# Windowed and neighbourhood attention in one layer: two heads split as one tile, attention output stored in parts and added by transfers, small operations on GpSimd

## The chip, the cores and the metric

The kernel runs on one core of a Trainium2 chip. The metric is device time in microseconds, measured over the whole program; the kernel before was run three times. Beside it stands one profiled execution, whose span is the time from its first to its last instruction. The engines are TensorE (PE in the profile, its weight loads PEld), VectorE (DVE), ScalarE (ACT), GpSimd (POOL) and SyncE (SP), which here only issues transfers.

## The reference

One layer of an encoder on 1024 tokens of 1024 channels, float32. What the change touches is the attention in its middle:

```python
h = x + 0.5 * swiglu(rms_norm(x), ...)
u = rms_norm(h)
qa, ka, va, qb, kb, vb, ga, gb = split(u @ w_in)
ya = neighbourhood_attention_2d(qa, ka, va, rpb)         # branch A: 8 heads of 64, window 8 x 16 on a 64-wide grid, learned bias
yb = windowed_gqa_sink(rope(qb), rope(kb), vb, sink)     # branch B: 8 heads, 2 key heads, |i - j| <= 128, sink logit in the denominator
merged = sigmoid(ga) * (ya @ w_branch_a) + sigmoid(gb) * (yb @ w_branch_b)
h = h + merged @ w_out
h = h + 0.5 * swiglu(rms_norm(h), ...)
y = rms_norm(h, final_norm)
```

Both attentions are a softmax over the window; in branch B `exp(sink)` is added to the sum of the exponentials, with no value behind it.

## The kernel before, in words

**Numbers in two parts.** Matmuls take float32r operands. A float32 operand is split into a high part (a ScalarE cast, L95) and the rest (a VectorE subtraction, L98), and a product is three matmuls: high x high, high x low, low x high (`mm3`, L149, L151, L153). The large products of the two feed-forward halves and of the input projection use one Strassen step each (`products`, `Down`).

**Stages.** First feed-forward half, input projection, attention, merge and output projection, second feed-forward half, final norm. Tokens are reordered on the host so that a block of 128 tokens is a compact piece of the grid; then each query block j needs the key blocks j-1, j and j+1 in both branches.

**A unit of attention.** A unit is one query block (128 tokens) for two heads. Branch B has 8 blocks x 4 pairs = 32 units, branch A 4 pairs x 8 blocks = 32 units, in this order. For a unit:

- `scores` (L1403): for each of the two heads two matmuls (L1417, L1418: queries times the high and low parts of the keys) into one PSUM bank of 384 columns (256 at the edge blocks). VectorE adds the bias or mask, negates and takes the running minimum (L1422), ScalarE takes the exponential and its sum (L1425). In branch B the negated sink logit is copied in as one column ahead of the scores (L1414 for both heads at once, or L1421 one by one in every third unit, whose buffers lie apart). Then VectorE takes the reciprocal of both sums (L1428) and scales one head (L1429), while ScalarE scales the other (L1430).
- `turn` (L1432): six transposes (L1438), three for each head's bank, then `split` of each bank (L95 on ScalarE, L98 on VectorE) into high and low probabilities.
- `values` (L1445): value matmuls into one bank `g` (L1457 for B, L1452 for A) and `write`. The values tile holds the high part in columns 0 to 63 and the low part in 64 to 127, so the upper 64 output partitions are a second addend: ScalarE copies it down (L1361, L1381) and VectorE adds (L1362; in A, where two probability parts give two results, L1382 and L1386 or L1392).

**Where y goes.** For branch B and for the first three head pairs of branch A the sum is stored to a DRAM buffer `y_d` (L1364 from GpSimd's queue, one transfer for a block; L1388 from SP's queue, one for four blocks) and fetched again as rows (`fetch_y`, L1253), then split into operands of the branch projections (`split_y`, L1255). The last head pair of A stays in the chip's memory.

**The order of the work.** A loop over n (L1476) interleaves the units as a pipeline: scores of unit n, some filler, transposes of unit n-2, some filler, values of unit n-3. The filler is a generator of other matmuls (remaining gate columns, then branch B's projection, then the first two tiles of branch A's); `filling` (L1463) takes a number of steps fixed by constants, a step being six 128x512 matmuls. `prep_a` loads the keys, queries and values of branch A's next head pair from GpSimd's queue (L1211, L1214) and SP's (L1221). From this program order a planner makes each engine's own order: it places an instruction by its estimate of when the operands will be there, so that loads go far ahead of their place in the text. Each engine and each queue then runs its list strictly in that order and waits on semaphores. Instructions marked with `pin` (in `split_y` the high cast, `late=True`) keep their program order on their engine. The first stage is ordered by hand and not touched.

**PSUM.** One pool of eight banks: four for tag `g`, four for tag `d`. `bank(tag)` hands out one bank of 512 columns in rotation. Scores take two `d` banks one after the other, transposes the next two.

Of the kernel before, what the change touches and what calls it, by code (L numbers as in the profile page):

```python
# [15 lines left out]
P = 128  # L16
# [6 lines left out]
HD = 64  # L23
# [13 lines left out]
def trunk_kernel(ctx, tc, x, xt, n1, wg1, wu1, wd1, nm, win, rpb, sink, wa, wb, wo,  # L37
# [11 lines left out]
    ps = ctx.enter_context(tc.tile_pool(name="ps", bufs=4, space=bass.MemoryType.PSUM))  # L49
    dram = ctx.enter_context(tc.tile_pool(name="dram", bufs=1, space=bass.MemoryType.DRAM))  # L50

    uid = [0]

    def nm_(s):
        uid[0] += 1
        return f"{s}_{uid[0]}"
# [3 lines left out]
    nhalf4 = const.tile([P, 4], F32, name="nhalf")  # L60
    nc.gpsimd.memset(nhalf4, -0.5)
    nhalf = nhalf4[:, 0:1]

# [16 lines left out]
    def bank(tag):  # L80
        return ps.tile([P, 512], F32, tag=tag, name=nm_(tag))

    def raw4():
        return main.tile([P, 1024], F32, tag="raw", bufs=4, name=nm_("raw"))
# [883 lines left out]
    u_d = dram.tile([4, P, 512], F32, name="u_d")  # L968
    y_d = dram.tile([D, T], F32, name="y_d")
    kept.append(u_d)  # L970
# [209 lines left out]

    drain(pg[2])
    mix["lo"] = main.tile([P, 512], F32, tag="s1", bufs=1, name=nm_("s1")).rearrange("p (k s t) -> p k s t", k=2, s=2)

# [67 lines left out]
    def fetch_y(r0):  # L1251
        mix["y", r0] = raw4()
        nc.sync.dma_start(mix["y", r0], y_d[r0:r0 + P, :])  # L1253

# [11 lines left out]
    def branch_a(i):  # L1266

        bs = [bank("dg"[i % 2]) for _ in range(2)]
        a_mm.append((bs, branch_mm(bs, mix.pop(("w", NC8 + i)), Y_A)))
# [83 lines left out]
    def units_b():  # L1353
        for j in range(NTT):
            for c in range(4):
                def write(o, j=j, c=c):

                    if c == 0:
                        ybox["b"] = xs4()[:HD].rearrange("p (c s t) -> p c s t", c=4, s=2)
                    lo = mix["lo"][:HD, c % 2]  # L1360
                    nc.scalar.copy(lo, o[HD:])  # L1361
                    nc.vector.tensor_tensor(ybox["b"][:, c], o[:HD], lo, op=ALU.add)  # L1362
                    if c == 3:
                        nc.gpsimd.dma_start(y_d[:512, j * P:(j + 1) * P].rearrange("(c s p) t -> p c s t", s=2, p=HD), ybox["b"])  # L1364

                g = c // 2
                yield dict(j=j, q=[qs_b(j)[:, 4 * s + c, :] for s in range(2)],
                           kd=[kd_b()[g]] * 2, kl=[kl_b()[g]] * 2, v=[mix["vb"][g]], bias=[mask_b] * 2,
                           sink=nsk[:, 2 * c:2 * c + 2], write=write)

    def units_a():
        for hp in range(4):
            qs, kd, kl, va = heads_a[hp]
            for j in range(NTT):
                def write(o, j=j, hp=hp):

                    if hp == 3 and j == 0:
                        ybox["a"] = new_fx(2)
                    y = fa[:, 3072:4096] if hp < 3 else ybox["a"]
# [4 lines left out]
                    if hp < 3:  # L1384
                        both = y[j // 4 * HD:j // 4 * HD + HD].rearrange("p (s t) -> p s t", s=2)
                        nc.vector.tensor_tensor(both[:, :, j % 4 * P:(j % 4 + 1) * P], o[:HD, :, 0, :], lo, op=ALU.add)  # L1386
                        if j in (3, 7):
                            nc.sync.dma_start(y_d[512 + hp * P:512 + (hp + 1) * P, cols].rearrange("(s p) t -> p s t", s=2), both)  # L1388
                        return
                    for s in range(2):  # L1390
# [12 lines left out]
    def scores(un):  # L1403
# [9 lines left out]
        if ext and not third:  # L1413
            nc.vector.tensor_copy(both[:, :, 0], un["sink"])  # L1414
        for s in range(2):
            b = bank("d")
            nc.tensor.matmul(b[:, :nw], un["q"][s], un["kd"][s][:, k0 * P:k1 * P], start=True, stop=False)  # L1417
            nc.tensor.matmul(b[:, :nw], un["q"][s], un["kl"][s][:, k0 * P:k1 * P], start=False, stop=True)  # L1418
            pr = held[4 + s][:, :ext + nw] if third else both[:, s, :ext + nw]
            if ext and third:  # L1420
                nc.vector.tensor_copy(pr[:, 0:1], un["sink"][:, s:s + 1])  # L1421
            nc.vector.tensor_tensor_reduce(out=pr[:, ext:], in0=b[:, :nw], in1=un["bias"][s][:, moff:moff + nw], scale=-1.0,  # L1422
# [4 lines left out]
        npair[0] += 1  # L1427
        nc.vector.reciprocal(rc, ssum)  # L1428
        nc.vector.tensor_scalar_mul(un["pr"][0], un["pr"][0], rc[:, 0:1])  # L1429
        nc.scalar.activation(un["pr"][1], un["pr"][1], AF.Copy, scale=rc[:, 1:2])  # L1430

    def turn(un):  # L1432
        nk = un["nk"]
        un["p"] = [ws4()[:, :768].rearrange("p (k s t) -> p k s t", k=3, s=2) for _ in range(2)]
        for s in range(2):
            pt = bank("d")
            for i in range(nk):
                nc.tensor.transpose(pt[:, i * P:(i + 1) * P], un["pr"][s][:, i * P:(i + 1) * P], ident)  # L1438
# [122 lines left out]


    gain = load_gain(n2[0])
    merge = down
# [65 lines left out]
    scale(NTT - 1)  # L1630


# [67 lines left out]
```

## Time and profile before

| | |
|---|---|
| time, median of 3 runs | 1917.81 us (1917.64 to 1918.79) |
| span of the profiled execution | 1915.6 us |
| TensorE, VectorE, ScalarE, GpSimd busy over the span | 99%, 76%, 49%, 16% |
| attention stage (first score to last value matmul) | 917 to 1161 us |
| bytes moved, whole span | 338.57 MB |

In the profile a row of a group names the line, engine and operation, what is written `<-` what is read, the shapes and the count; then the busy time of the group in us and the mean duration of one in ns; then the idle time of the engine just before such instructions and who ended it. Durations of consecutive instructions of one engine can overlap by some tens of ns. Matmul ends are modelled.

### The profile page before, as it was taken

Reading aid. Unit: us, or ns where it says so; the run is one execution under the profiler, and the core shown is the slowest. Engines: PE = TensorE matmul, PEld = TensorE weight load, DVE = VectorE, ACT = ScalarE, POOL = GpSimd, SP = SyncE. Lnnn points to the kernel's source line nnn. Section 1 sums busy time; section 2 is a strip of 40 time slices with the busy share of each in tenths; the row PEclk is TensorE's granted clock in tenths of the full one; section 3 lists DMA queues with packets and bytes.
Section 4 is the critical chain, followed back from the end, with each engine's and each line's share of the span. In section 5 each row is a group of like instructions: output and inputs, shape, how many; then the busy total and the mean of one; then the engine's idle time right before and its main releaser. Section 6 shows DMA issues by size and latency. Waiting matters only on the chain.

```text
span 1915.6 us, 25959 instructions
## 1 busy us (share of the span) xinstructions
PE 1905.7 (99%) x9044; PEld 1597.7 (83%) x9044; DVE 1451.9 (76%) x2545; ACT 947.5 (49%) x1847; POOL 306.5 (16%) x477
## 2 busy tenths in 40 slices
PE   9999999999999999999999999999999999999998
PEld 7888888888888888898898888888888888888886
DVE  8988766668967778755887997999675566569864
ACT  7533444444446543444888983475333333344453
POOL 0012222214400112211112201010110001005111
PEclk9999999999999999999999999999999999999999
DMA  7256656677354277753648978444432323492341
GB/s 269 95 175 217 231 200 219 205 277 284 115 180 141 105 213 236 226 176 127 176 117 228 283 225 309 171 154 133 142 110 97 118 88 110 157 357 86 119 140 61
DMA packets 174211, 338.57 MB, mean 177 GB/s; under 512 B 17280, under 2 KB 79616, under 8 KB 174080
## 3 DMA queue, kind: packets, MB, share of 16 engines
q1 hardware_dynamic: 140752, 235.18, 37.5%
q0 software_dynamic: 32464, 100.69, 15.6%
q8 instruction: 71, 1.16, 0.3%
q10 hardware_dynamic: 864, 1.05, 0.2%
q14 instruction: 60, 0.49, 0.1%
HBM read 230.43 MB, written 108.19 MB: 177 GB/s over the span
## 4 chain that ended last, share of the span: by engine, by line
PE 97%; DVE 1%; DMA 1%; ACT 0%; issue 0%; POOL 0%; SPq 0%; POOLq 0%; DVEq 0%; ACTq 0%
PE g L149 18%; PE g L153 17%; PE g L151 17%; PE d L153 12%; PE d L151 12%; PE d L149 12%; PE d L1438 2%; PE g L1457 1%; PE d L1417 1%; PE g L1452 1%; PE d L1418 1%; PE d L142 1%; DVE ar L98 0%; DMA fx<-in_xt_dram 0%; DMA fx<-v_d 0%
## 5 line engine op out<-in xcount | busy, mean ns | idle before, releaser
L149 PE MATMUL g<-ar,ws 128*128 128x512 f32 x1064 | 404.6, 393 | 0.0
L151 PE MATMUL g<-ar,ws 128*128 128x512 f32 x1064 | 401.8, 390 | 0.0
L153 PE MATMUL g<-ar,ws 128*128 128x512 f32 x1064 | 400.4, 390 | 0.0
L149 PE MATMUL d<-ar,ws 128*128 128x512 f32 x728 | 281.6, 390 | 0.4 <-ACT ar L908 0.4
L151 PE MATMUL d<-ar,ws 128*128 128x512 f32 x728 | 281.1, 389 | 0.6 <-DVE ar L910 0.6
L153 PE MATMUL d<-ar,ws 128*128 128x512 f32 x728 | 281.2, 389 | 0.0
L153 PEld LDWEIGHTS g<-ar,ws 128*128 128x128 f32 x1064 | 199.6, 188 | 41.6
L151 PEld LDWEIGHTS g<-ar,ws 128*128 128x128 f32 x1064 | 199.6, 188 | 41.0
L149 PEld LDWEIGHTS g<-ar,ws 128*128 128x128 f32 x1064 | 196.6, 188 | 35.9 <-DVE fa L1030 0.3
L332 DVE TENSOR_TENSOR ws<-raw,ws 128x512 fp32r<-128x512 f32 x216 | 147.6, 688 | 92.9 <-ACT ws L325 92.0
L325 ACT CAST ws<-raw 128x512 fp32r<-128x512 f32 x216 | 132.6, 620 | 149.6 <-PE g L153 67.0
L151 PEld LDWEIGHTS d<-ar,ws 128*128 128x128 f32 x728 | 136.7, 188 | 29.8 <-DVE ar L910 1.2
L149 PEld LDWEIGHTS d<-ar,ws 128*128 128x128 f32 x728 | 136.5, 188 | 28.9 <-ACT ar L908 0.9
L153 PEld LDWEIGHTS d<-ar,ws 128*128 128x128 f32 x728 | 136.6, 188 | 28.7 <-DVE ws L332 0.5
L95 ACT CAST ws<-raw 128x512 fp32r<-128x512 f32 x98 | 61.0, 623 | 119.2 <-PE d L153 59.9
L98 DVE TENSOR_TENSOR ws<-raw,ws 128x512 fp32r<-128x512 f32 x98 | 73.2, 747 | 44.3 <-ACT ws L95 44.2
L444 POOL DMA_DIRECT2D hid<-fx x91 | 49.2, 540 | 349.6 <-DVE fx L504 221.6
L98 DVE TENSOR_TENSOR ws<-ar,ws 128x512 fp32r<-128x512 f32 x114 | 93.5, 828 | 14.6 <-ACT ws L95 14.6
L95 ACT CAST ar<-raw 128x512 fp32r<-128x512 f32 (+1 forms) x81 | 54.0, 670 | 83.5 <-PE g L151 51.5
L149 PE MATMUL g<-ws,ws 128*128 128x512 f32 x232 | 90.9, 392 | 0.0
L153 PE MATMUL g<-ws,ws 128*128 128x512 f32 x232 | 90.4, 390 | 0.0
L151 PE MATMUL g<-ws,ws 128*128 128x512 f32 x232 | 90.3, 389 | 0.0
(344 smaller groups left out, 3830.9 us busy)
## 6 DMA issues: line engine op xcount, KB each, us to landing
raw<-hid SPq DMA_DIRECT2D x70, 512.0 KB
hid<-fx POOLq DMA_DIRECT2D x91, 256.0 KB, 2.7
ar<-in_ffn_w_down_dram SPq DMA_DIRECT2D x32, 512.0 KB
raw<-in_ffn_w_up_dram SPq DMA_DIRECT2D x31, 512.0 KB
raw<-in_ffn_w_gate_dram SPq DMA_DIRECT2D x27, 512.0 KB
hid<-fa POOLq DMA_DIRECT2D x51, 256.0 KB, 2.7
ar<-zs_d POOLq DMA_DIRECT2D x48, 256.0 KB, 7.5
raw<-in_w_in_dram SPq DMA_DIRECT2D x20, 512.0 KB
```

Of the source, the lines that this page charges most:

```text
L95: hi = nc.scalar.copy(dst_hi, src)
L98: (eng or nc.vector).tensor_tensor(dst_lo, src, f32v(dst_hi), op=ALU.subtract)
L142: nc.tensor.transpose(pt[:, c * P:(c + 1) * P], xs[:, (half * 4 + c) * P:(half * 4 + c + 1) * P], ident)
L149: nc.tensor.matmul(b, lhs[0], r[0], start=first, stop=False, **kw)
L151: nc.tensor.matmul(b, lhs[0], r[1], start=False, stop=False, **kw)
L153: nc.tensor.matmul(b, lhs[1], r[0], start=False, stop=last, **kw)
L325: nc.scalar.copy(w[0][:, :512], a)
L332: nc.vector.tensor_tensor(w[0][:, 512:], a, f32v(w[0][:, :512]), op=ALU.subtract)
L444: nc.gpsimd.dma_start(hid[PRODUCTS.index(p), i], src)
L1417: nc.tensor.matmul(b[:, :nw], un["q"][s], un["kd"][s][:, k0 * P:k1 * P], start=True, stop=False)
L1418: nc.tensor.matmul(b[:, :nw], un["q"][s], un["kl"][s][:, k0 * P:k1 * P], start=False, stop=True)
L1438: nc.tensor.transpose(pt[:, i * P:(i + 1) * P], un["pr"][s][:, i * P:(i + 1) * P], ident)
```

## The change

- The `d` banks move into a second PSUM pool, which is closed and opened again: as four single banks before and after attention, and as two tiles of two banks during attention. The two heads of a unit take the two halves of one tile, in `scores` and in `turn`.
- In branch B the probabilities of both heads are split by one ScalarE copy and one VectorE subtraction over both banks (768 columns) instead of one pair for each head.
- `y_d` gets three layers. Branch B's `write` is now a single ScalarE copy of all 128 partitions; every fourth one issues two transfers, of the upper and the lower 64 partitions, into layers 0 and 1. For the first three head pairs of branch A `write` is one ScalarE copy and one VectorE copy into one of two small boxes, and three transfers from SP's queue into layers 0, 1 and 2, for each block. `fetch_y` loads layer 0 from SP's queue and adds the other layers (one for B, two for A) by accumulating transfers on GpSimd's queue.
- The reciprocal is now a power of -1 on GpSimd; the copies of the sink column are on GpSimd.

```diff
+    second = {}
+    def open_second(pairs):
+        if second:
+            second["guard"].__exit__(None, None, None)
+        second["guard"] = tc.tile_pool(name=f"pd{len(second)}{int(pairs)}", bufs=2 if pairs else 4,
+                                       space=bass.MemoryType.PSUM, reuse_waits="tile")
+        second["pool"] = second["guard"].__enter__()
...
+    none2 = const.tile([P, 2], F32, name="none")
+    nc.gpsimd.memset(none2, -1.0)
+    open_second(False)
...
+    def two_banks():
+        t = second["pool"].tile([P, 1024], F32, tag="d", name=nm_("d"))
+        return t.rearrange("p (s k) -> p s k", s=2)
...
-    y_d = dram.tile([D, T], F32, name="y_d")
+    y_d = dram.tile([3, D, T], F32, name="y_d")
...
     drain(pg[2])
+    open_second(True)
...
     def fetch_y(r0):
-        mix["y", r0] = raw4()
-        nc.sync.dma_start(mix["y", r0], y_d[r0:r0 + P, :])
+        r = mix["y", r0] = raw4()
+        nc.sync.dma_start(r, y_d[0, r0:r0 + P, :])
+        for k in range(1, 2 if r0 < 512 else 3):
+            nc.gpsimd.dma_start(r, y_d[k, r0:r0 + P, :], accum_op=ALU.add)
...
-        bs = [bank("dg"[i % 2]) for _ in range(2)]
+        bs = [bank("g") for _ in range(2)] if i % 2 else [b for b in two_banks().rearrange("p s k -> s p k")]
...
-                        ybox["b"] = xs4()[:HD].rearrange("p (c s t) -> p c s t", c=4, s=2)
-                    lo = mix["lo"][:HD, c % 2]
-                    nc.scalar.copy(lo, o[HD:])
-                    nc.vector.tensor_tensor(ybox["b"][:, c], o[:HD], lo, op=ALU.add)
+                        ybox["b"] = xs4().rearrange("p (c s t) -> p c s t", c=4, s=2)
+                    nc.scalar.copy(ybox["b"][:, c], o)
                     if c == 3:
-                        nc.gpsimd.dma_start(y_d[:512, j * P:(j + 1) * P].rearrange("(c s p) t -> p c s t", s=2, p=HD), ybox["b"])
+                        for k in range(2):
+                            nc.gpsimd.dma_start(y_d[k, :512, j * P:(j + 1) * P].rearrange("(c s p) t -> p c s t", s=2, p=HD),
+                                                halves(ybox["b"])[k])
...
+                    if hp < 3:
+                        box = fa[:, 3072 + j % 2 * 512:][:, :512].rearrange("p (k s t) -> p k s t", k=2, s=2)
+                        nc.scalar.copy(box[:, 0], o[:, :, 0, :])
+                        nc.vector.tensor_copy(box[:HD, 1], o[:HD, :, 1, :])
+                        for k, part in enumerate((box[:HD, 0], box[HD:, 0], box[:HD, 1])):
+                            nc.sync.dma_start(y_d[k, 512 + hp * P:512 + (hp + 1) * P, j * P:(j + 1) * P]
+                                              .rearrange("(s p) t -> p s t", s=2), part)
+                        return
...
-            nc.vector.tensor_copy(both[:, :, 0], un["sink"])
+            nc.gpsimd.tensor_copy(both[:, :, 0], un["sink"])
+        banks = two_banks()
         for s in range(2):
-            b = bank("d")
+            b = banks[:, s]
...
-                nc.vector.tensor_copy(pr[:, 0:1], un["sink"][:, s:s + 1])
+                nc.gpsimd.tensor_copy(pr[:, 0:1], un["sink"][:, s:s + 1])
...
-        nc.vector.reciprocal(rc, ssum)
+        nc.gpsimd.tensor_tensor(rc, ssum, none2, op=ALU.pow)
...
+        banks = two_banks()
         for s in range(2):
-            pt = bank("d")
+            pt = banks[:, s]
...
-            else:
-                dst = [un["p"][k][:, :nk, s, :] for k in range(2)]
-            split(dst[0], dst[1], pt[:, :nk * P].rearrange("p (k t) -> p k t", k=nk))
+                split(dst[0], dst[1], pt[:, :nk * P].rearrange("p (k t) -> p k t", k=nk))
+        if len(un["v"]) == 1:
+            hi, lo = [p[:, :nk].rearrange("p k s t -> p s k t") for p in un["p"]]
+            split(hi, lo, banks[:, :, :nk * P].rearrange("p s (k t) -> p s k t", k=nk))
...
+    open_second(False)
     gain = load_gain(n2[0])
```

The matmuls, their count, and the numbers of filler steps are the same in both kernels.

More of the change, by code (lines that the diff above doesn't have):

```diff
@@ L80, in bank @@
     def bank(tag):
-        return ps.tile([P, 512], F32, tag=tag, name=nm_(tag))
+        return (ps if tag == "g" else second["pool"]).tile([P, 512], F32, tag=tag, name=nm_(tag))
+    def two_banks():
+        t = second["pool"].tile([P, 1024], F32, tag="d", name=nm_("d"))
+        return t.rearrange("p (s k) -> p s k", s=2)
     def raw4():
@@ L1375, in write @@
                 def write(o, j=j, hp=hp):
-                    if hp == 3 and j == 0:
+                    if hp < 3:
[6 more added lines that the diff above has]
+                        return
+                    if j == 0:
                         ybox["a"] = new_fx(2)
-                    y = fa[:, 3072:4096] if hp < 3 else ybox["a"]
+                    y = ybox["a"]
                     lo = mix["lo"][:HD, j % 2]
@@ L1383, in write @@
                     cols = slice((j - 3) * P, (j + 1) * P)
[L1384 to L1389, printed above, removed]
                     for s in range(2):
@@ L1630, in trunk_kernel @@
     scale(NTT - 1)
+    second["guard"].__exit__(None, None, None)
 def _consts():
```

## The prediction

> **What bounds the kernel now.** I read the page first, then the chain of waits, then the stretch in which the changed lines run.
>
> ```profile
> span 1915.6 us, 25959 instructions
> PE 1905.7 (99%) x9044; PEld 1597.7 (83%) x9044; DVE 1451.9 (76%) x2545; ACT 947.5 (49%) x1847; POOL 306.5 (16%) x477
> PE 97%; DVE 1%; DMA 1%; ACT 0%; issue 0%; POOL 0%; SPq 0%; POOLq 0%; DVEq 0%; ACTq 0%
> ```
>
> TensorE is busy 99% of the span and carries 97% of the chain that ended last. Attention runs from the first score matmul at 917 us to the last value matmul at 1161 us. The windows view of its two halves, branch B and branch A (time, then busy time and count by engine, granted clock, DMA share, GB/s):
>
> ```profile
> 917.00:1035.00 118.00, 117.99 (x728) 105.20 (x728) 98.68 (x342) 101.47 (x275) 21.18 (x37) 1.00 0.54 151
> 1035.00:1161.00 126.00, 125.73 (x754) 110.50 (x753) 112.48 (x338) 105.46 (x267) 14.46 (x27) 1.00 0.93 271
> ```
>
> VectorE and ScalarE are 80 to 90% busy here and TensorE all but fully. The ends of matmuls are modelled, so busy time can hide short stalls; the waits view of the same stretch (engine and line, whom it waited for, us in total, times, longest) gives them for TensorE and its weight loads, complete:
>
> ```profile
> PEld d L1438 <- DVE ws L98: 1.6, 6, 0.4
> PEld d L1417 <- DVE nmx L1422: 0.8, 3, 0.3
> PEld d L1438 <- DVE nmx L1422: 0.3, 1, 0.3
> PEld g L149 <- DVE xs L1362: 0.2, 1, 0.2
> PE d L1438 <- DVE ws L98: 0.2, 1, 0.2
> ```
>
> Sum: 3.1 us. The change takes away no matmul and no transpose (the same loops issue the same 1482 in this stretch), so 3.1 us, 0.16% of 1917.81, is all that relieving other engines can give. A measurement of this kernel can tell about 0.2%, 3.8 us, from no change. That is the first result: little can be won; the question is what can be lost.
>
> The profiled execution has a span of 1915.6 us. The three runs gave 1917.64 to 1918.79, so about 2.2 us lie around the span; I add the sum to the median, 1917.81.
>
> **The rhythm that the edits must fit.** Branch B, one unit after another (start, us, engine, line):
>
> ```profile
> 962.47 0.34 PE L1417 MATMUL d<-ar,ar 128*128 128x384 f32 x1
> 965.93 0.34 PE L1417 MATMUL d<-ar,ar 128*128 128x384 f32 x1
> 966.20 0.17 DVE L1428 RECIPROCAL rc<-ssum 128x2 f32<-128x2 f32 x1
> 966.43 0.63 ACT L1430 ACTIVATE hs<-hs,rc 128x384 f32<-128x384 f32 x1
> 967.86 0.62 ACT L1425 ACTIVATE fa<-fa,nmx 128x385 f32<-128x385 f32 x1 [0.41 <-DVE nmx L1422]
> 968.02 0.82 PE L1438 MATMUL d<-ident,fa 128*128 128x128 f32 x6
> 970.25 0.55 DVE L98 TENSOR_TENSOR ws<-d,ws 128x384 fp32r<-128x384 f32 x1
> 971.48 0.71 PE L1438 MATMUL d<-ident,hs 128*128 128x128 f32 x5
> ```
>
> A unit takes 965.93 - 962.47 = 3.46 us. The scores of 962.47 are scaled by 966.43 + 0.63 = 967.06 and transposed at 971.48: 4.4 us of slack for the data. The engines' order is tighter. Transposes of 968.02 are read out by 970.25 + 0.55 = 970.80 and the next want their banks at 971.48: 0.68 us. ScalarE idles 0.41 us a unit, before 967.86. So an instruction that holds up ScalarE by more than 0.41 + 0.68 = 1.1 us holds up TensorE too.
>
> **The edits, one by one.** The rows for VectorE and ScalarE, from the groups of 917 to 1161 (busy us in all, mean ns):
>
> ```profile
> L98 DVE TENSOR_TENSOR ws<-d,ws 128x384 fp32r<-128x384 f32 x96 | 51.2, 551 | 6.9 <-ACT ws L95 6.3
> L98 DVE TENSOR_TENSOR ar<-raw,ar 128x1024 fp32r<-128x1024 f32 x8 | 9.8, 1221 | 0.1
> L95 ACT CAST ws<-d 128x384 fp32r<-128x384 f32 x96 | 43.7, 478 | 6.2 <-PE d L1438 5.2
> L95 ACT CAST ar<-raw 128x1024 fp32r<-128x1024 f32 x7 | 7.3, 1050 | 0.0
> L1362 DVE TENSOR_TENSOR xs<-g,s 64x256 f32<-64x256 f32 x32 | 13.2, 412 | 1.2 <-ACT s L1361 0.9
> L1428 DVE RECIPROCAL rc<-ssum 128x2 f32<-128x2 f32 x64 | 10.5, 164 | 12.0 <-ACT fa L1425 6.1 <-ACT hs L1425 4.9
> L1414 DVE COPY fa<-nsk 128x2 f32<-128x2 f32 x20 | 3.2, 159 | 0.0
> ```
>
> *The split of two heads as one.* A subtraction of 768 columns, between the 384 and 1024 rows, is 551 + (1221 - 551) x 384/640 = 953 ns; two cost 1102. Likewise the copy: 821 for 956 ns. The 32 units of B save 4.8 us of VectorE and 4.3 us of ScalarE. Against it, the copy waits for all six transposes, 968.02 + 0.82 = 968.84, and reads out at 968.84 + 0.82 + 0.95 = 970.6 if both engines are free: as late as the 970.80 of today. Cost to TensorE 0; if an exponential (0.62 us) slips in ahead of the copy it ends at 971.2, still before 971.48. The two-bank tile also makes the first score matmul wait for both heads' bias steps instead of one; today's wait there is 0.8 us in all (L1417), and VectorE gets emptier. The hand-over at the start can cost up to the last eviction of the stage before:
>
> ```profile
> 917.05 0.28 PE L1417 MATMUL d<-ar,ar 128*128 128x256 f32 x1
> 917.58 0.68 DVE L1030 SCALAR_TENSOR_TENSOR fa<-d,fa 128x512 f32<-128x512 f32 x1
> ```
>
> If the first pair of banks holds that one, scores start at 918.3: 0 to 1.2 us, once; I take 0.5.
>
> *The y parts.* VectorE loses the 32 additions of L1362 (13.2 us). Of branch A's first 24 units it loses two additions of L1362's shape, 0.41 us each, and gains a copy of that shape, at most 0.41: 9.9 us less. With the reciprocals (10.5), the sink copies of L1414 (3.2; those of L1421 are smaller) and the split (4.8), VectorE gives up some 42 of 211 us. TensorE's 3.1 us are waits on VectorE; I take half of them as gone: -1.5 us.
>
> *Reciprocals on GpSimd.* The same operation stands elsewhere as L131, the nearest row for a sink copy is L130 (ns minimum/median/maximum):
>
> ```profile
> L131 POOL TENSOR_TENSOR st<-st,nhalf x20: 567/568/897, 581.1 to 1862.9; 128x1 f32<-128x1 f32 x20
> L130 POOL TENSOR_SCALAR st<-st x20: 220/222/944, 580.8 to 1862.3; 128x1 f32<-128x1 f32 x20
> ```
>
> Each reciprocal comes 568 - 164 = 404 ns later, at worst 897 - 164 = 733. Both are under the 1.1 us above; cost 0. Its cover is ScalarE's idle time, and if all 64 x 0.40 = 26 us landed on ScalarE it would be at 207 - 4 + 26 = 229 of 244 us. GpSimd takes 64 x 0.57 = 36 us and some 40 copies of 0.22 = 9 us more, beside 21 + 14 = 35 today.
> The Trainium skill, "SBUF — State Buffer", section "Who interferes with whom", says that a VectorE operation in a two-port mode locks GpSimd out for its whole length. By it the in-place scale of L1429 could hold a reciprocal for its own duration, and the loss would still be 0; no run here shows it.
>
> But reciprocals now stand in GpSimd's queue among DMA issues, which come in bursts:
>
> ```profile
> 1053.03 2.10 POOL L1211 DMA_DIRECT2D ar<-zs_d  x4 [10.68 <-PE d L1417]
> 1055.07 1.10 POOL L1214 DMA_DIRECT2D ar<-zs_d  x2
> 1082.97 2.25 POOL L1211 DMA_DIRECT2D ar<-zs_d  x4 [16.00 <-PE d L1418]
> ```
>
> A burst of six lasts 2.10 + 1.10 = 3.2 us, and a second one starts the same way. A reciprocal caught in the middle is 1.6 us late, plus 0.4, minus 1.1: 0.9 us of TensorE. Two bursts with one caught in one of them: between 0 and 2 x (3.2 + 0.4 - 1.1) = 5.0, I take +0.9.
>
> *Sums by transfer.* Bytes: B's stores 2.1 MB more, its loads 2.1, A's stores 3.1 (72 of 64 KB for 6 of 256 KB), A's loads 3.1, in all 10.4 MB, over 8 of them after 1035 us, where 34 MB move at a DMA share of 0.93. Transfers there will land later than now. Landings that I can read (KB, us) and the two places with least time:
>
> ```profile
> y_d<-xs POOLq DMA_DIRECT2D x8, 256.0 KB, 3.9
> ar<-zs_d POOLq DMA_DIRECT2D x48, 256.0 KB, 7.5
> 1042.83 0.33 SPq L1253 DMA_DIRECT2D raw<-y_d  x1
> 1052.10 1.04 ACT L95 CAST ar<-raw 128x1024 fp32r<-128x1024 f32 x1
> 1133.39 0.32 SPq L1253 DMA_DIRECT2D raw<-y_d  x1
> 1149.18 1.04 ACT L95 CAST ar<-raw 128x1024 fp32r<-128x1024 f32 x1
> ```
>
> These casts are held in program order on ScalarE, so one that waits stops the exponentials behind it. B: load 3.9, issue 0.55, accumulation 3.9 (7.5): 1051.2 (1054.8) against 1052.10, 0 to 2.7 us late. A's third head pair: two more store issues of 0.6 (row below), 1134.6; load 3.9, two accumulations of 0.55 + 3.9 (7.5): 1147.4 (1154.6) against 1149.18, 0 to 5.4 late. I take 0 for both, since the 3.9 is the same tensor's.
> The Trainium skill, "DMA: Bandwidth & Descriptors", section "Anatomy of one DMA — SWDGE (gpsimd) path", gives 2.0 us plus bytes/436e9; for 512 KB an estimate of 3.2 us from that page, by which both would be in time as well. The 7.5 us row contradicts it where transfers crowd.
>
> A's small stores: the box is used again two units later, in A 2 x 126/32 = 7.9 us.
>
> ```profile
> L1388 SPq DMA_DIRECT2D y_d<-fa x6: 586/587/2757, 1055.6 to 1129.8; - x6
> 1101.27 5.38 SPq L1221 DMA_DIRECT2D fx<-v_d  x3
> ```
>
> Copy on ScalarE at most 0.48 (the L95 row of more columns), copy on VectorE 0.41, three issues of 0.587 and a landing of 3.9: 6.6 us, so 1.3 in hand. Cost 0, unless such a row of L1221 stands ahead in SP's queue.
>
> **Sum.** -1.5 + 0.5 + 0.9 = -0.1 us; with a little lateness that I can't place, +0.4: **1918.1 us**, no change that can be told. Its own ends: -3.1 to +1.2 + 5.0 - 1.5, that is 1914.7 to 1922.5.
>
> **The rivals.** The slower ones come on top of 1918.1.
>
> *GpSimd waits on a transfer (slower).* Ten accumulations must wait for their load, or for the accumulation before, in the queue in which the reciprocals stand. If the planner puts one ahead of a reciprocal and the transfer lands at 7.5 instead of 3.9 us, ScalarE's scale is 3.6 + 0.4 - 1.1 = 2.9 us too late. It decides from the point at which a landing is 0.7 us behind the plan. Three of ten: +8.7, **1926.8**. For it: DMA share 0.93. Against: a planner that orders by readiness puts most reciprocals first. 0.20.
>
> *ScalarE waits on y (slower).* The upper ends above, less 1.1 each: 1.6 + 4.3 = 5.9, **1924.0**. For: the same crowding. Against: by 1130 us the transfers thin out. 0.11.
>
> *Boxes behind SP (slower).* Stores behind 5.4 us of L1221, twice: 2 x (5.4 - 1.3 - 1.1) = 6.0, **1924.1**. 0.10.
>
> *All waits go (faster).* -3.1 from 1917.8, **1914.7**; still within 0.2%. For it: all five rows name VectorE. 0.08. To be faster by over 3.8 us the matmul stream itself would have to thin out, which nothing in the change does: 0.04 of these at most.
>
> **How the numbers follow.** Forecast 0.51. The three slower rivals, 0.41, end above the bound of 1921.6 with nine in ten of their chance, 0.37, and the forecast's upper end adds 0.03: slower 0.40, faster 0.04, same 0.56. The range goes from the end that loses all waits, 1914.7, to the dearest rival, 1926.8; the forecast's own is 1914.7 to 1922.5.
>
> **What would show it.** Right: TensorE's busy time again at 1905 to 1906 us; VectorE down by some 42 us between 917 and 1161; L1438's waits on L98 under 1.6 us; reciprocals on POOL at about 0.57 us, with ScalarE's waits for them up by less than 26 us. Wrong: TensorE or its loads waiting on ScalarE for several us (then the ScalarE rows say whether rc, y_d or a store ended the wait), or an attention stage that is longer than 244 us with full queues on SP.

## The result, and the profile after

The kernel after takes 1974.12 us (median of 5 runs, 1972.81 to 1975.75) where the kernel before takes 1917.64 in the same session (5 runs, 1917.49 to 1918.79): a ratio of 1.0293, interval 1.0281 to 1.0306, slower by 56 us. The prediction said no change, 1918.1, with a range that ended at 1926.8.

The page of the kernel after, first the span, then the busy time of the engines, then the chain that ended last:

```profile
span 1974.0 us, 26137 instructions
PE 1928.2 (98%) x9044; PEld 1599.7 (81%) x9044; DVE 1424.5 (72%) x2351; ACT 942.9 (48%) x1815; POOL 374.9 (19%) x602
PE 88%; DMA 5%; DVE 2%; ACT 2%; issue 1%; POOL 1%; SPq 0%; POOLq 0%; DVEq 0%; ACTq 0%
```

The same 9044 matmuls run, VectorE has 27 us less to do (1451.9 before), and TensorE's share of the chain fell from 97% to 88%: transfers, VectorE, ScalarE and GpSimd have 10% of it instead of 2%. The windows view of the two halves of attention, with the columns as before, shows where:

```profile
917.00:1035.00 118.00, 113.45 (x666) 94.89 (x664) 73.88 (x187) 89.89 (x221) 49.95 (x105) 1.00 0.49 138
1035.00:1217.00 182.00, 151.10 (x812) 121.13 (x812) 109.55 (x302) 112.73 (x288) 53.05 (x80) 0.94 1.01 258
```

In the first 118 us TensorE starts 666 matmuls instead of 728. Branch B's last value matmul, at 1035 us before, starts at 1046, and branch A's, at 1160 before, at 1217: 11 us are lost in B's half and 46 in A's. The granted clock in A's half, 1.00 before, is 0.94. The waits view of 900 to 1215 us:

```profile
POOL raw L1272 <- DMA raw<-y_d: 29.4, 6, 11.7
...
PEld d L1439 <- DVE nmx L1444: 26.7, 44, 7.0
DVE fa L1451 <- POOL rc L1450: 26.1, 24, 4.6
ACT fa L1452 <- POOL rc L1450: 24.3, 25, 5.2
ACT fa L1398 <- DMA y_d<-fa: 19.6, 8, 7.8
...
PEld d L1461 <- DVE ws L114: 17.9, 25, 6.1
```

TensorE still waits for VectorE's bias step (L1444) and split (L114), as before, but for 45 us instead of 2.4 in these two rows. VectorE itself has become emptier, so it must have been held up, and the other four rows name by what: reciprocals on GpSimd (L1450), a box whose store has not landed (L1398 writes it), and accumulations queued behind transfers (L1272).

### The profile page after: what moved, and what is told of

It is laid out like the page before. It is cut to its first block, busy times and chain, and to the rows that moved or that the text cites. A ratio compares the mean times of both kernels' runs of the same rounds, so it can differ in the third digit from the quotient of the medians.

```text
span 1974.0 us, 26137 instructions
## 1 busy us (share of the span) xinstructions
PE 1928.2 (98%) x9044; PEld 1599.7 (81%) x9044; DVE 1424.5 (72%) x2351; ACT 942.9 (48%) x1815; POOL 374.9 (19%) x602
## 4 chain that ended last, share of the span: by engine, by line
PE 88%; DMA 5%; DVE 2%; ACT 2%; issue 1%; POOL 1%; SPq 0%; POOLq 0%; DVEq 0%; ACTq 0%
PE g L165 16%; PE g L169 16%; PE g L167 16%; PE d L165 12%; PE d L169 12%; PE d L167 12%; DMA y_d<-fa 3%; DMA raw<-y_d 1%; POOL rc L1450 1%; PE d L1461 1%; ACT fa L1447 1%; PE d L158 1%; PE d L1439 1%; ACT ws L111 1%; DVE fa L1444 1%
## 5 line engine op out<-in xcount | busy, mean ns | idle before, releaser
L165 PE MATMUL g<-ar,ws 128*128 128x512 f32 x1064 | 409.2, 394 | 4.7 <-DVE fa L1399 4.6
L167 PE MATMUL g<-ar,ws 128*128 128x512 f32 x1064 | 404.9, 391 | 0.2 <-DVE ar L114 0.2
L169 PE MATMUL g<-ar,ws 128*128 128x512 f32 x1064 | 404.9, 392 | 0.0
L114 DVE TENSOR_TENSOR ws<-raw,ws 128x512 fp32r<-128x512 f32 x98 | 73.5, 750 | 44.2 <-ACT ws L111 44.2
L114 DVE TENSOR_TENSOR ws<-ar,ws 128x512 fp32r<-128x512 f32 x114 | 93.6, 828 | 15.2 <-ACT ws L111 15.2
```

What stands on the lines that cost most here:

```text
L114: (eng or nc.vector).tensor_tensor(dst_lo, src, f32v(dst_hi), op=ALU.subtract)
L165: nc.tensor.matmul(b, lhs[0], r[0], start=first, stop=False, **kw)
L167: nc.tensor.matmul(b, lhs[0], r[1], start=False, stop=False, **kw)
L169: nc.tensor.matmul(b, lhs[1], r[0], start=False, stop=last, **kw)
```

## The experiments

Theory: engines stand in their queues behind late transfers and behind GpSimd. Rivals: one part alone is to blame; the parts cost only together; or the order shifts and no wait matters. Times are medians; a ratio is to the kernel before on the same chip, whose median lay between 1917.85 and 1918.76.

### Each part alone on the kernel before

**Reciprocals and sink copies.**

```diff
...
-        nc.vector.reciprocal(rc, ssum)
+        nc.gpsimd.tensor_tensor(rc, ssum, none2, op=ALU.pow)
...
```

> The kernel before with only the reciprocals and the sink copies moved to GpSimd. Theory Q (each engine stands in its own queue behind a late transfer or behind GpSimd; the loss needs the accumulating transfers and the two boxes of branch A): nothing but the later reciprocal is left, 0.7 instead of 0.16 us, which fits into the gaps of branch B or nearly so: 1918 to 1923. Rival R (the reciprocal's way through GpSimd is itself the loss, through the 54 us that VectorE and ScalarE wait for it in the changed kernel): 1930 to 1970, in both halves of attention.

Measured: 1939.16 us, 1.0107 (1.0092 to 1.0122).

**Branch A's y in parts**: the change's `write` for A, and `fetch_y` with two accumulations for A's rows and none for B's.

> The kernel before with only branch A's y in parts: two boxes, three small stores a block from SP's queue, two accumulating loads for each of three head pairs. Theory Q: the two boxes hold ScalarE until their stores have landed, and most of the 56 us is here even with the reciprocals on VectorE: 1940 to 1960, all of it in the second half of attention, with ScalarE waiting for y_d for 15 us or more. Rival R: below 1925.

Measured: 1949.26 us, 1.0164 (1.0147 to 1.0181).

**Branch B's y in parts**: the change's `write` for B, and one accumulation for B's rows.

> The kernel before with only branch B's y in parts: one copy instead of copy and addition, two stores a block from GpSimd's queue, one accumulating load for each of four. Theory Q: the accumulating loads hold nothing that is needed soon, as no reciprocal stands behind them: 1916 to 1921. Rival (the pinned casts of y on ScalarE come too early for the accumulated data): 1922 to 1930, with ScalarE waiting for y_d or raw near 1050 us.

Measured: 1926.57 us, 1.0040 (1.0025 to 1.0055).

**Two-bank tiles with the merged split.** All that is left of the change.

> The kernel before with only the two-bank tiles and the common split in branch B. Theory Q: 1916 to 1920, as the banks come free as early as before. Rival (the coarser banks make TensorE wait, as L1439 waited 26.7 us for the bias steps in the changed kernel): 1925 to 1940, with that wait in both halves.

Measured: 1930.45 us, 1.0063 (1.0048 to 1.0078).

Every part costs by itself: 20.9 + 31.0 + 8.3 + 12.2 = 72 us alone, 56 together. The rival of a single culprit is out, and so is that of parts that cost only together.

### Why the reciprocals cost 21 us

The timeline of the kernel with the reciprocals alone on GpSimd, in branch B (start, us, engine, line; idle time before and its releaser in brackets):

```profile
962.16 0.62 ACT L1427 ACTIVATE fa<-fa,nmx 128x385 f32<-128x385 f32 x1
...
963.01 0.72 POOL L1430 TENSOR_TENSOR rc<-ssum,none 128x2 f32<-128x2 f32 x1 [1.57 <-ACT fa L1427]
...
963.76 0.62 ACT L1432 ACTIVATE fa<-fa,rc 128x384 f32<-128x384 f32 x1 [0.90 <-POOL rc L1430]
963.76 0.42 DVE L1431 TENSOR_SCALAR fa<-fa,rc 128x384 f32<-128x384 f32 x1 [1.18 <-POOL rc L1430]
```

Here the next instruction of both engines needs the reciprocal, and both stand for about 1 us. The planner puts the scales right behind the exponentials, where a reciprocal of 0.17 us fitted. Over the whole stage:

```profile
DVE fa L1431 <- POOL rc L1430: 27.6, 32, 1.8
ACT fa L1432 <- POOL rc L1430: 18.8, 33, 1.3
DVE hs L1431 <- POOL rc L1430: 11.4, 14, 1.8
ACT hs L1432 <- POOL rc L1430: 7.9, 16, 0.9
```

VectorE stands for 39.0 us, ScalarE for 26.7. Before, VectorE stood for 11.0 us at the reciprocal itself (the row of L1428 in the prediction), and ScalarE hardly waited for it:

```profile
ACT fa L1430 <- DVE rc L1428: 3.1, 13, 0.3
...
ACT hs L1430 <- DVE rc L1428: 0.6, 2, 0.3
```

So the rise is 28.0 us on VectorE and 23.0 on ScalarE. If that is the cause, something else to do in the meantime must cure it. So the scales were put half a unit later, with the reciprocals left on GpSimd (pinned: it stays behind what is written ahead of it for its engine):

```diff
+            if s == 0:
+                scale_late()
...
-        nc.vector.tensor_scalar_mul(un["pr"][0], un["pr"][0], rc[:, 0:1])
-        nc.scalar.activation(un["pr"][1], un["pr"][1], AF.Copy, scale=rc[:, 1:2])
+            pin(nc.vector.tensor_scalar_mul(pr[0], pr[0], rc[:, 0:1]))
+            pin(nc.scalar.activation(pr[1], pr[1], AF.Copy, scale=rc[:, 1:2]))
```

> Reciprocals and sink copies on GpSimd, alone on the kernel before (1939.16 us), with the two scales that use a reciprocal put half a unit later in VectorE's and ScalarE's order, behind the first bias step and the first exponential of the next unit. Theory H (VectorE and ScalarE stand at the head of their queues until the reciprocal is there, some 0.6 us in every unit against 0.4 us of idle time that ScalarE has in each): most of the 20.9 us come back, 1918 to 1928, and the waits on the reciprocal (66 us on both engines together) fall under 15 us. Rival L (the reciprocal's lateness reaches the transposes as data, or GpSimd's other work holds it): 1934 to 1945.

Measured: 1919.80 us, 1.0010 (1.0001 to 1.0019); 19 of the 21 us are back. Of the two scales' waits on the reciprocal 3.8 us are left, in three rows. The largest:

```profile
DVE fa L1439 <- POOL rc L1433: 2.2, 5, 0.7
```

The control, the same late scales with the reciprocals on VectorE:

> The control for the late scales: the kernel before, reciprocals and sink copies on VectorE as they were, only the two scales half a unit later. Theory H: no change, 1916 to 1920, so that the 19 us which the late scales gave with reciprocals on GpSimd came from the waits alone. Rival: the later place itself shifts the order and gains or costs more than 3 us.

Measured: 1918.43 us, 1.0001 (0.9991 to 1.0010). The later place is free by itself. So it was the standing that cost, not GpSimd's work nor the age of the data: with the late scales GpSimd still computes every reciprocal, and the scaled data come later still. This point is shown.

In the kernel after, the part was undone in the same two ways. First, reciprocals and sink copies back on VectorE:

> The kernel after, with the 64 reciprocals and the copies of the sink column back on VectorE; nothing else changed. Alone on the kernel before, this part cost 20.9 us. Theory A (each part costs by itself, in part the same microseconds twice): it takes 5 to 21 us back, 1953 to 1969; the other three parts alone cost 31.0 + 8.3 + 12.2 = 51.5, so 1969.8 if those add up fully. Rival G (GpSimd waits on the accumulating transfers with the reciprocals behind them, so that the reciprocals carry the interplay too): over 25 us back, under 1949. Rival N (the late transfers hide the reciprocals' lateness): under 4 us back, over 1970.

Measured: 1960.07 us (1957.20 to 1963.45), 14 us back. Then the late scales:

> The kernel after, with the two scales that use a reciprocal half a unit later in VectorE's and ScalarE's order; the reciprocals stay on GpSimd, beside its accumulating transfers. Theory H (what the reciprocals cost in the kernel after is the standing of VectorE and ScalarE at the head of their queues): about what putting them back on VectorE gave, 14 us back, 1956 to 1965. Rival G (the accumulating transfers hold GpSimd's queue for several us, longer than half a unit): 1967 to 1975, with the waits on the reciprocal still there.

Measured: 1964.44 us (1961.01 to 1967.67), 10 us back. One row of its waits view, and from its timeline what stands right ahead of the reciprocal in the longest of these waits:

```profile
DVE fa L1459 <- POOL rc L1453: 15.5, 11, 4.5
...
1104.85 0.94 POOL L1272 DMA_DIRECT2D raw<-y_d  x1 [6.66 <-DMA raw<-y_d]
```

Waits of up to 4.5 us are longer than half a unit, so rival G holds in part: some reciprocals stand behind an accumulation, which itself waits in GpSimd's queue for the load before it. The two spans of runs overlap, so the 4 us between them are not told apart from nothing.

### Why the two-bank tiles cost 12 us

The waits of TensorE's weight loads with the tiles alone, where the kernel before had 0.8 and 1.6 us:

```profile
PEld d L1433 <- DVE nmx L1438: 8.2, 32, 0.4
PEld d L1455 <- DVE ws L112: 6.8, 26, 1.2
```

Small waits, none over 1.2 us, but in nearly every second unit. Is it the merged split or the pair? Branch B split head by head, in pair tiles:

> The two-bank tiles alone on the kernel before (1930.45 with the merged split), now with branch B split head by head as before, so that only the tiles differ. Theory T (both banks of a pair come free together, and so later): the loss stays, 1927 to 1934, in both halves. Rival M (the merged split, which waits for all six transposes): the loss goes, 1917 to 1921.

Measured: 1931.00 us, 1.0070 (1.0053 to 1.0086). The loss stays, so it is the tiles; merging the split in them costs nothing that can be told. Then a pair for the scores alone, with single banks for the transposes:

> The pair tile for the scores alone on the kernel before; transposes and splits keep their two single banks (pairs for both: 1931.0 us). Theory T (each pair comes free late: TensorE's weight loads wait 8.2 us on the bias step for the scores and 6.8 us on the split for the transposes): about half the 13 us stays, 1922 to 1928. Rival S1 (the scores' pair carries all): 1928 to 1932. Rival S2 (the transposes' pair carries all): 1917 to 1920.

Measured: 1924.16 us, 1.0031 (1.0019 to 1.0043), half of the loss, with this row:

```profile
PEld d L1433 <- DVE nmx L1438: 9.6, 39, 0.4
```

The scores' pair costs 6 us, which leaves 6 to 7 for the transposes' by difference; their pair was not tried alone. What the pair does is in the timeline of the same kernel: the score matmul of a unit's first head, the end of this head's bias step, and the score matmul of the second head.

```profile
950.13 0.34 PE L1433 MATMUL d<-ar,ar 128*128 128x384 f32 x1
...
951.23 0.09 DVE L1438 DVE_READ_ACCUMULATOR2_ANT nmx<- 128x1 f32 x1
...
951.37 0.44 PE L1433 MATMUL d<-ar,ar 128*128 128x384 f32 x1
```

The second head's matmuls write the other bank, and yet they start only when the first head's bank has been read. In the kernel before, the second head follows the first by 0.35 us (962.82 after 962.47), and in all 64 units its weight load starts ahead of the end of the first head's bias step, in the median by 1.5 us. With the scores' pair it never does, and in 47 of 64 units it starts 0.05 to 0.08 us behind that end. So in this program a tile of two banks is waited for as a whole, and its two heads run one behind the other at VectorE's pace. Branch A's transposes, split head by head, show the same in the kernel with pairs for both: the second head's start when the first head's split has ended (in one unit 1085.96 after 1085.91).

### Why branch B's parts cost 8 us

The chain of waits of the kernel with B's parts alone, around its one long stall (start, us, what):

```profile
1038.85 6.46 DMA y_d<-xs
...
1045.49 3.73 DMA raw<-y_d
...
1049.88 9.12 DMA raw<-y_d
...
1059.03 1.05 ACT ar L95
...
1062.05 0.58 PE d L1419
```

The load began at 1045.49, not at 1042.83 as before, because the stores of B's last block, issued at 1038.85, landed only 6.46 us later. It took 3.73 us, as estimated (3.9); the accumulation behind it took 9.12 where 3.9 (7.5) had been allowed. The pinned cast L95 waited 5.45 us and with it ScalarE's exponentials. Would a later cast save it? The four splits were put one or two filler steps later:

```diff
-                                     3: lambda: split_y(Y_B[0], 0, nc.vector),
-                                     4: lambda: [split_y(Y_B[1], P, nc.vector), fetch_y(3 * P)],
-                                     5: lambda: fetch_gate(1),
-                                     6: lambda: split_y(Y_B[2], 2 * P, nc.vector)})
+                                     4: lambda: fetch_y(3 * P),
+                                     5: lambda: [split_y(Y_B[0], 0, nc.vector), fetch_gate(1)],
+                                     6: lambda: split_y(Y_B[1], P, nc.vector)})
...
```

> Branch B's y in parts alone on the kernel before (1926.57 us), with the four splits of the fetched rows one or two filler steps later, close ahead of their use. Theory C (the high cast keeps its place on ScalarE and waits 5.4 us for a late accumulation while the exponentials stand behind it): the wait goes, 1917 to 1922. Rival R (the accumulations are late for branch B's projection too, or the DMA engines are the limit): 1924 to 1930.

Measured: 1931.78 us, 1.0073 (1.0058 to 1.0088). Theory C fell: the wait did go, and the time went up by 5 us. Two other transfers are waited for longer instead (1.7 and 1.6 us in the same rows with the early splits):

```profile
ACT xs L1287 <- DMA xs<-g_d: 7.8, 1, 7.8
...
PE g L149 <- DMA ws<-wab_d: 3.5, 1, 3.5
```

### Why branch A's parts cost 31 us

Waits of the kernel with A's parts alone:

```profile
PEld g L149 <- DVE fa L1382: 18.8, 3, 8.9
...
ACT fa L1381 <- DMA y_d<-fa: 16.4, 5, 8.6
...
DVE fa L1382 <- DMA y_d<-fa: 15.7, 5, 9.1
```

The copies into a box wait for the store of the box two units earlier; VectorE stands, and TensorE waits for a bank. Its two long stalls, 8.58 us up to 1070.62 and 8.45 up to 1117.14, lie behind two stores in the chain of waits:

```profile
1049.48 3.90 DMA y_d<-fa
...
1055.81 14.25 DMA y_d<-fa
...
1101.02 15.14 DMA y_d<-fa
```

A store of 64 KB that landed after 3.90 us in the beginning, as the prediction had assumed, took 14 to 15 us there, counted from its issue. That names the boxes, so four were made of the two, alone and in the kernel after:

```diff
-                        box = fa[:, 3072 + j % 2 * 512:][:, :512].rearrange("p (k s t) -> p k s t", k=2, s=2)
+                        box = fa[:, 3072 + j % 4 * 256:][:, :256].rearrange("p (s t) -> p s t", s=2)
+                        low = mix["lo"][j % 2 * HD:j % 2 * HD + HD, j % 4 // 2]
...
```

> Branch A's y in parts alone on the kernel before (1949.26 with two boxes), now with four boxes. Theory B: TensorE's two stalls of 8.8 and 8.7 us, with the slower matmuls right behind each (2.0 and 2.3 us), go: 21.8 of the 31.0 us, 1924 to 1932. Rival S (SP's queue and the number of transfers): the stalls stay behind another transfer, 1938 to 1950.

> The kernel after, with four boxes in turn for branch A's parts instead of two (same columns of fa, and the free lo tile for the third part); same stores, same copies, same transfers. Theory B (the copies into a box wait for the store of the box two units earlier): ScalarE's waits on y_d<-fa (19.6 us) and VectorE's on it fall under 5 us, and 20 to 30 us come back, 1944 to 1954. Rival G (GpSimd's waits on the accumulations set the pace): under 8 us back, 1966 to 1974. Rival S (SP's queue and the number of transfers set the pace, and the waits move to the next load): 1960 to 1974 with the waits on another transfer.

Measured: 1948.33 us alone, 1.0155 (1.0140 to 1.0170), and 1978.41 in the kernel after (1976.79 to 1980.59). Theory B fell: next to nothing alone, 4 us more in the whole. In the first of them a fetched gate and an accumulation hold ScalarE instead:

```profile
ACT xs L1287 <- DMA xs<-g_d: 14.0, 1, 14.0
...
ACT ar L95 <- DMA raw<-y_d: 11.8, 2, 10.9
```

So the waits move on to the next transfer. Theory D followed: no time is left on the DMA engines. First the loads and the stores were tried apart:

> The kernel before with branch A's two accumulating transfers for each of the three fetches alone: y is stored summed and once, as before, and the fetch adds the same layer twice more (so that branch A's y comes in threefold for those channels). It adds the loads of the parts, not their stores. Theory D (the DMA engines have no time left: before, they are busy 93% of 1035 to 1161 us, 8 us of 125 free; worked out from the packets and shares of the queues, the accumulations of A take about 10 us of all 16 engines, the small stores about 19): 1920 to 1929. Rival P (GpSimd's queue and the late casts of y carry the loss of the A parts, 31.0 us): 1935 to 1950.

> The kernel before with branch A's stores in parts alone (two copies and three small stores for each block, into three layers); the fetch loads layer 0 only, so the output lacks the other two layers. Theory D: the small stores take about 19 us of the DMA engines, 8 of them free before: 1929 to 1938, with waits on whichever load comes late. Rival P: under 1922.

Measured: accumulations alone 1925.69 us, 1.0044 (1.0027 to 1.0061); stores alone 1942.44, 1.0126 (1.0111 to 1.0141). 7.5 + 24.2 = 31.7 for 31.0: the small stores carry three quarters, more than theory D's 20 at most. Then stores of every second block:

```diff
+                        for k, part in enumerate((box[:HD], box[HD:], low) if j % 2 else ()):
```

> Branch A's y in parts alone (1949.26 us; 1948.33 with four boxes), the same bytes in the same three layers, but stored every second block: 36 stores of 128 KB in runs of 1 KB instead of 72 of 64 KB in runs of 512 bytes. Theory D with a cost for each packet (41 ns for 512 bytes, 61 ns for 1 KB, from the shares and counts of the queues before and with the parts): the stores take 6 us less of the DMA engines, 1938 to 1945. Rival B (bytes alone count, or the casts' waits): 1946 to 1952.

Measured: 1942.26 us, 1.0125 (1.0110 to 1.0140): 7 us back. That fits theory D and its cost of a packet, but it fits half as many issues on SP too, and a box here is used again after four blocks instead of two. The last pair took other transfers away and left the boxes and their queues alone:

```diff
-        r = mix["rb", dc] = xs4() if dc % 3 else masks[:, :1024]
-        nc.sync.dma_start(r, g_d[D + dc * P:D + (dc + 1) * P, :])
+        r = mix["rb", dc] = masks[:, :1024]
+        if dc == 0:
+            nc.sync.dma_start(r, g_d[D + dc * P:D + (dc + 1) * P, :])
```

> Branch A's y in parts alone on the kernel before (1949.26 us), with seven of the eight fetches of branch B's gate left out (512 KB each, 3.7 of some 32 MB that move between 1035 and 1160 us; the one fetched gate serves all eight tiles, so the merge is computed with the wrong gates). Boxes, stores, accumulations and their queues are untouched. Theory D (the DMA engines have no time left in this stretch, and whichever transfer is late stops TensorE): 3.7 MB at 255 to 270 GB/s are some 14 us of the engines, of which 8 to 18 us of time come back, 1931 to 1941. Rival B (the boxes' own chain of copy, issue, landing and reuse, or the accumulations one behind the other, whatever else moves): 1944 to 1950.

> The same seven fetches left out of the kernel after (1974.12 us; the merge is computed with the wrong gates). Theory D: 8 to 18 us come back, 1956 to 1966. Rival B: 1968 to 1975.

Measured: 1958.36 us alone (1956.44 to 1960.09), 9 us more than with all fetches, and 1978.97 in the kernel after (1975.63 to 1981.93). Theory D fell in this form. The stretch of branch A in the windows view, with A's parts alone:

```profile
1035.00:1161.00 126.00, 106.54 (x609) 92.91 (x608) 82.88 (x256) 86.89 (x229) 17.84 (x31) 0.92 1.00 256
```

and with seven fetches fewer:

```profile
1035.00:1161.00 126.00, 103.25 (x577) 89.56 (x576) 78.22 (x242) 81.29 (x217) 17.99 (x31) 0.91 0.90 214
```

The DMA share fell from 1.00 to 0.90 and the bytes by a sixth, and TensorE started fewer matmuls still. The two long stalls did get shorter, from 8.58 and 8.45 to 6.30 and 6.87 us, but others of 4.16 and 6.10 came, so full engines alone are not shown to be the cause. (The gates' one tile also changes what their activations wait for, so this edit is not clean, and a small gain on the DMA engines could be hidden in it.) What else the traces show is SP's queue. SP's waits on transfers from 1035 to 1180 us, first before:

```profile
SPq L1253 <- DMA y_d<-fa: 11.4, 3, 4.5
...
SPq L1253 <- DMA y_d<-xs: 6.0, 1, 6.0
```

then with A's parts alone, the three largest rows of its stores:

```profile
SPq L1384 <- DMA raw<-y_d: 6.5, 2, 3.6
...
SPq L1384 <- DMA fa<-bm_d: 5.0, 2, 3.3
...
SPq L1384 <- DMA y_d<-fa: 4.2, 3, 1.6
```

Before, almost only the fetch of a y waits, for y's own store. Now stores wait in SP's queue 20 us for transfers, most of them ones with which they share no data (biases, values, rows of y that are not theirs), and what stands behind them in the queue waits too. Over all lines SP's waits on transfers in this stretch rose from 18.6 to some 31 us. 72 issues at the 0.58 us of a single one are 42 us of SP's time besides. This was not tried by itself (other queues for the stores, say). So it is shown that the many small stores cost 24 of the 31 us, that the two long stalls wait for stores which land 14 to 15 us after their issue, that neither more boxes nor fewer other bytes win the time back, and that fewer and longer stores do in part. What makes the landings so long, and whether SP's queue or the order that the planner makes sets the rest, stays open; so the rival that the order shifts is not out for the parts of y.

## Why the prediction was wrong

*What bounds the kernel, and that little can be won*: held. Nothing of the 1.5 us taken for a less busy VectorE can be seen. Of the 42 us that it was to give up, its busy time shows 27. The working was right all the same: the durations of its instructions around attention (905 to 1262 us before, 905 to 1320 after) add up to 362.8 and 320.2 us, and busy time counts their overlapping ends once.

*The margin of 1.1 us.* This step failed. It was the sum of 0.41 us of ScalarE's idle time, which comes back in every unit, and 0.68 us that a bank has in hand, which can be spent once. A lateness that comes in all 64 units has the 0.41 alone. GpSimd's power took 0.71 us for two columns (0.57 had been taken from a row of one), 0.55 more than the reciprocal's 0.16, and VectorE, which had the reciprocal from itself, now gets it from another engine. The loss measured, 20.9/64 = 0.33 us a unit, is small; times 64 it is the second largest term. Of it, 0.55 - 0.41 = 0.14 us a unit, 9 us in all, would follow from ScalarE's idle time; VectorE's standing, up by 28 us, had no price at all, and how the rest divides is not shown. That up to 26 us could land on ScalarE was a fair estimate (its waits rose by 23.0), but it was then compared with ScalarE's idle time over the whole stage, as if an engine could save its idle time up.

*"The two-bank tile also makes the first score matmul wait for both heads' bias steps ... today's wait there is 0.8 us in all"*, cost 0. This step failed. The wait that came is another one, of the second head's matmuls for the first head's bias step in the same unit, and the price was read from a kernel in which that wait does not exist. It became about 6 us for the scores and, by difference, as much again for the transposes, where a pair was not priced for the heads of branch A. That the merged split itself costs nothing was right: its subtraction takes 955 ns for 953 worked out.

*"I take 0 for both"* (late accumulations, then pinned casts). The mechanism was right, the landing mis-sized: 9.1 us, not 3.9, and 8.3 us of time for B. The 3.9 is the row of B's stores of 256 KB; a load or an accumulation moves 512 KB. The load, too, began 2.7 us later than was reckoned. The bound of 7.5 us from the crowded transfers of the same stretch was the better row; it was quoted and passed over. The estimate of 3.2 us that the prediction took from the Trainium skill, "DMA: Bandwidth & Descriptors", section "Anatomy of one DMA — SWDGE (gpsimd) path", is contradicted by the 9.12 us of the chain. For A's loads alone it is 7.5 us of time.

*Boxes: "1.3 in hand", cost 0; rival 6.0.* 24 us for the stores. This step is the largest term that failed: the chain was made of single durations at their usual size, 3.9 us for the landing, and in the two long stalls the landing took 14.25 and 15.14 us. The landings in a stretch with a DMA share of 0.93 and the 72 issues in one queue with all loads were named, and only the boxes' own place in it was priced, not what 66 further issues do to everything behind them. Which of the two made the landings long stays open.

*The rivals.* Two of the three slower ones are in the kernel after: GpSimd's wait, the likeliest, with 29.4 us in one row, and the boxes' with 19.6, though with A's parts alone the long stalls lay behind late landings and not behind L1221. ScalarE's wait on y, 6.3 us with B's parts alone, is 0.2 there. Each was priced as two or three events of a few microseconds, and each was taken to come alone: the upper end of the range, 1926.8, is the dearest rival and not a sum, although nothing in the mechanisms excludes one another.

*What would show it wrong* named the right signs: ScalarE's rows show the reciprocal and the stores, and the stage is longer. The signs of being right failed: TensorE's busy time is 1928.2 us, its weight loads wait 17.9 us for the split, and a reciprocal takes 0.71 us.

## What to carry to other kernels

Where one engine is busy 99% of the time, ask of every edit whether its lateness comes once or in every round: only slack that is renewed in each round pays for the second kind, and the price is the rest times the number of rounds. When a producer moves to a slower engine, move its consumers later in their queues too; here that was worth 19 of 21 us. Before putting two results into one tile over two banks, ask whether the second writer must then wait for the first reader; here it did. Before splitting a transfer into many small ones, count their issues and their landings in the busiest stretch of the queue they will share, since the next load in it pays if the store does not.

## What the runs showed of the hardware

In the kernel with A's parts alone TensorE came back at half speed after its first long stall, of 8.58 us. A row of two matmuls just before this stall and just behind it:

```profile
1060.28 0.62 PE L151 MATMUL g<-ar,ws 128*128 128x512 f32 x2
...
1070.62 0.79 PE L149 MATMUL g<-ar,ws 128*128 128x512 f32 x1 [8.58 <-DVE fa L1382]
1071.21 1.05 PE L151 MATMUL g<-ar,ws 128*128 128x512 f32 x2
```

and the windows view of the same places, with the granted clock in the third column from the end:

```profile
1056.00:1061.00 5.00, 5.00 (x33) 4.48 (x32) 4.59 (x15) 3.05 (x10) 0.87 (x2) 1.00 1.15 258
1070.62:1075.50 4.88, 4.88 (x16) 4.30 (x17) 2.10 (x7) 3.27 (x7) 2.68 (x6) 0.50 0.79 257
1075.50:1080.00 4.50, 4.50 (x27) 3.94 (x26) 4.43 (x12) 3.60 (x9) 0.50 (x1) 1.00 1.16 245
```

At 0.50 for 4.9 us, some 2.4 us are lost on top of the 8.6 of the stall: this wait cost over a quarter more than it lasted. The Trainium skill, "TensorE: Matmul & The Clock Gate", section "What's actually happening", says that the array's clock is halved after an idle window of about 3.4 us and full again after one such busy window. The trace agrees on the half, 0.50, and on an idle time of 8.58 us being enough; the half speed lasted 4.9 us here, longer than one such window.

An accumulating transfer of 512 KB took 5.2 to 9.7 us to land in the kernel after, median 7.4, and 0.90 us to issue on GpSimd, where a plain load of the same bytes on SP's queue landed in 3.7 us in the chain above. That the adding makes the difference is not shown: plain loads of 256 KB on GpSimd's queue (`ar<-zs_d`) have a median of 7.7 us in the same kernel.

```profile
L1272 POOL DMA_DIRECT2D raw<-y_d x10: 873/903/941, 1059.8 to 1191.2; - x10
...
DMA to landing us min/median/max: 5.2/7.4/9.7
```
